# A hybrid decoder layer on one core: TensorE's auxiliary work put in program order and placed by counted turns

## The chip, the cores and the metric

The kernel runs on one core of one Trainium2 chip. The metric is the device time of one execution in microseconds (us); lower is better. In the profile PE is TensorE's matmul, PEld its weight load, DVE is VectorE, ACT is ScalarE, POOL is GpSimd and SP is SyncE, which here issues nearly all DMAs.

## The reference

One decoder layer on 256 tokens of width 2048, all float32. An RMSNorm and one wide input projection feed two mixers side by side: a Mamba-2 state space mixer (32 heads of 64, four groups with a state of 128, one chunk of 256 tokens) and a sparse attention (16 heads of 128, four key/value heads, compressed, selected and window branches). An output projection, a residual and a feed-forward block with a causal convolution follow. Inside the state space mixer xdt is x times dt, and cb holds the products of c and b.

```python
h = rms_norm(x, mix_norm_w[l])
proj = h @ w_in[l]
z, xbc, dt_raw, q, kc, vc, ksl, vsl, kwn, vwn, gl = jnp.split(proj, split_at, axis=-1)
xbc = jax.nn.silu(causal_depthwise_conv(xbc, ssm_conv_w[l], ssm_conv_b[l]))
xs, bm, cm = jnp.split(xbc, [D_SSM, D_SSM + SSM_GROUPS * SSM_STATE], axis=-1)
dt = jax.nn.softplus(dt_raw.astype(jnp.float32) + ssm_dt_bias[l].astype(jnp.float32))
y_ssm = ssd_chunked(xs.reshape(bsz, L, SSM_HEADS, SSM_HEAD_DIM), dt, ssm_a_log[l], ssm_d[l],
                    bm.reshape(bsz, L, SSM_GROUPS, SSM_STATE), cm.reshape(bsz, L, SSM_GROUPS, SSM_STATE))
y_ssm = rms_norm(y_ssm * jax.nn.silu(z), ssm_norm_w[l])
y_attn = nsa_attention(q.reshape(bsz, L, N_HEADS, HEAD_DIM), kv_shape(kc), kv_shape(vc),
                       kv_shape(ksl), kv_shape(vsl), kv_shape(kwn), kv_shape(vwn),
                       gl.reshape(bsz, L, 3, N_HEADS), cmp_pos_k[l], cmp_w1_k[l], cmp_w2_k[l],
                       cmp_pos_v[l], cmp_w1_v[l], cmp_w2_v[l])
y_attn = rms_norm(y_attn, attn_norm_w[l])
x = x + jnp.concatenate([y_attn, y_ssm], axis=-1) @ w_out[l]
h = rms_norm(x, ffn_norm_w[l])
u = causal_depthwise_conv(h @ w_up[l], ffn_conv_w[l], ffn_conv_b[l])
gate, val = jnp.split(u, 2, axis=-1)
x = x + (jax.nn.silu(gate) * val) @ w_down[l]
return rms_norm(x, final_norm_w)
```

## The kernel before

**The stream.** All large products are cut into steps. A step has one weight tile of 128x1024 floats: a DMA on SP's queue brings it (`raw`, four buffers), ScalarE rounds it to a high part (`whi`, line 338), VectorE takes the rest (`wlo`, line 344), and TensorE multiplies both parts. In the input projection a step is 24 matmuls of 256 columns, 16 with `whi` (line 368) and 8 with `wlo` (line 372); four steps make one pair of 128-channel outputs, which land in two of four `mm` banks of PSUM. In the output projection a step is 12 matmuls of 512 columns (lines 403 and 407). The plan of the input projection is b0 b1 c0 c1 x0 dt x1 ... x7, then the attention's keys and values, then q and z. The weights of a step are prepared three steps ahead (`AHEAD`), loads are issued seven ahead (`LOADS`).

**Evacuation.** When a pair is done its `post` runs. For b, c and x it is `conv_ssm` for each of the two channels: `u = mm * gate` (line 386, the root mean square of the input's tokens is in `gate`), one ScalarE multiply into `acc` (line 502), three VectorE multiply-adds (line 504), then a SiLU on ScalarE (line 531 for b and c, line 601 for x, where it writes `xs`). [...]

**Auxiliary work.** Between steps the loop calls `tick`, which advances the first of a queue of generators by so many yields: 2 for each step of b, c, dt and x, 1.45 for q and z, 1.5 for the state space mixer's later part (`R_SSM`, `RATE`). The generators hold the small products and transposes that run on TensorE between steps of the stream: `cb_group` (c.b for one group), `dt_softplus`, `make_xdt` (eight transposes of `xs` and a multiply by dt; the two token tiles t each with a bank of its own), `ssm_heads`, `attention(g)` (scores, softmax, transposes `trans` at line 835, products `pv` at lines 848 to 854, for t = 0 and 1), `split_attn` and `split_ssm`, and `x1_block`'s transposes after each quarter of the output projection (line 1024). A token's sum of squares is turned into a reciprocal root in `token_rsqrt` and `root_x`/`spread_root`.

**Order.** Instructions of each engine run in the order in which they stand in its queue. In the first six steps (while `pin` is set) that order is the program's. After it a list scheduler orders each engine's instructions; it hoists parts of an auxiliary burst into the matmul stream, and puts others back.

**The start.** Steps 0 to 2 are built with the transposes of x. `square_x(2)` stands behind step 3, `square_x(3)` and `root_x` behind step 4, `make_params` (six transposes of parameter rows, copied to `prm` and `dcol`) behind step 5, `spread_root` (the two products that fill `gate`) behind step 6, and there `pin` is cleared. The evacuation of b0 is put off from step 3 to step 6. `FILL` warm-up matmuls stand ahead of the first step.

Of the kernel before, what the change touches and what calls it, by code (L numbers as in the profile page):

```python
# [10 lines left out]
F32 = mybir.dt.float32  # L11
# [14 lines left out]
NHID = 256  # L26
NSH = 32
EPS = 1e-6
AHEAD, LOADS, WARM, FILL = 3, 7, 7, 4
RAWS, SPLITS, LATE = 4, 4, 4  # L30
R_SSM = 1.5
RATE = {"b": 2, "c": 2, "dt": 2, "x": 2, "ck": 1, "cv": 1, "q": 1.45, "z": 1.45}
PLAN = "b0 b1 c0 c1 x0 dt x1 x2 x3 x4 x5 x6 x7 kc0 kc1 vc0 vc1 ks0+ks1|ck vs kw0+kw1|cv vw " \
       "q0 q1 q2 q3 z0 z1 q4 q5 z2 z3 q6 q7 z4 z5 z6 z7"
NEG = -1e30
SCALE = 128 ** -0.5

# [5 lines left out]
def hymba_kernel(  # L43
# [6 lines left out]
    nc = tc.nc  # L50
# [12 lines left out]
    def big(slot, shape, dtype, name):  # L63
        return gp.tile(shape, dtype, tag=f"G{slot}", name=name)
# [13 lines left out]
    class Pinned:  # L78


        def __init__(self, eng):
            self.eng = eng

        def __getattr__(self, name):
            fn = getattr(self.eng, name)
            if not pin:
                return fn
            return lambda *a, **kw: tc.keep_in_program_order(fn(*a, **kw))  # L88

    pin = []  # L90
    V, A, T = Pinned(nc.vector), Pinned(nc.scalar), Pinned(nc.tensor)

    def split(hi, lo, src):
        A.activation(hi, src, AF.Copy)
# [330 lines left out]
    def dt_softplus(t80):  # L425
        dw = big(31, [NSH, 4, L], F32, "dtw")
        xb, m, z2, p_ = (dw[:, i] for i in range(4))
        ow = big(32, [NSH, 2, L], F32, "dtw2")
        e, ones_r = ow[:, 0], ow[:, 1]
        V.memset(ones_r, 1.0)  # L430
        A.activation(xb, t80[0:32], AF.Identity, bias=dtb)
        V.tensor_scalar(m, xb, 0.0, None, op0=ALU.max)
        A.activation(e, xb, AF.Abs)
        yield
        A.activation(e, e, AF.Exp, scale=-1.0)
        tc.keep_in_program_order(nc.scalar.activation(nA, nA, AF.Exp))
# [12 lines left out]
        yield  # L449
        V.scalar_tensor_tensor(p_, p_, 1.0, e, op0=ALU.add, op1=ALU.mult)  # L450
        V.scalar_tensor_tensor(m, p_, 2.0, m, op0=ALU.mult, op1=ALU.add)
        V.tensor_scalar(xb, m, nA, None, op0=ALU.mult)
        V.tensor_tensor_scan(e, ones_r, xb, 0.0, op0=ALU.mult, op1=ALU.add)
        A.dma_start(acum_d, e)
        yield
        ps = aux_bank()
        for t in range(NT):
            b = t * 144
            sl = slice(t * P, (t + 1) * P)
            T.transpose(ps[:, b:b + 32], m[:, sl], ident[0:32, 0:32])  # L460
            T.transpose(ps[:, b + 32:b + 64], e[:, sl], ident[0:32, 0:32])
            T.transpose(ps[:, b + 64:b + 144], t80[0:80, sl], ident[0:80, 0:80])
        pv = ps[:, 0:288].rearrange("p (t c) -> p t c", t=2)
        V.tensor_copy(tokp[:, :, 0:64], pv[:, :, 0:64])
        A.activation(gates, pv[:, :, 96:144], AF.Exp, scale=-1.0)
        V.tensor_scalar(gates, gates, 1.0, None, op0=ALU.add)
        V.reciprocal(gates, gates)
        V.tensor_scalar(gates[:, 0, 0:16], gates[:, 0, 0:16], t31, None, op0=ALU.mult)
        yield
# [41 lines left out]
    def cb_group(g):
        if g % 2 == 0:
            cbt.append(big(29 + g // 2, [P, 2, 384], F32, f"cbt{g // 2}"))
        for st in range(2):
            ps = aux_bank()
            b_ = bc[g][:, 0, :, st * P:(st + 1) * P]
            T.matmul(ps, b_[:, 0], bc[g][:, 1], start=True, stop=False)
            T.matmul(ps[:, 256:512], b_[:, 1], bc[g][:, 1, 0], start=False, stop=True)
            rt = t256("rt")
            cv = cbt[g // 2][:, g % 2]  # L520
            n = L - st * P
            A.activation(rt[:, :n], ps[:, 256 + st * P:512], AF.Copy)
            V.tensor_tensor(cv[:, 256 * st:256 * st + n], ps[:, st * P:256], rt[:, :n], op=ALU.add)
            V.tensor_tensor(cv[:, 256 * st:256 * st + P], cv[:, 256 * st:256 * st + P], tri, op=ALU.mult)
            yield

    def bc_evac(which, g0):
        def evac(c, ps):
            g = g0 + c
            acc = conv_ssm(ps, 16 + which * 4 + g)  # L530
            A.activation(acc, acc, AF.Silu)
            split(bc[g][:, which, 0], bc[g][:, which, 1], acc)
            if which == 1:
                aux.append(cb_group(g))
        return evac


# [3 lines left out]
    def make_xdt(i):  # L541
        xd = big(16 + i, [P, NT, 512], F32, f"xdt{i}")
        xdt.append(xd)
        for t in range(NT):
            ps = aux_bank()
            for j in range(4):
                T.transpose(ps[:, j * P:(j + 1) * P], xs[i][:, j, t * P:(t + 1) * P], ident)
            V.tensor_tensor(xd[:, t].rearrange("p (h e) -> p h e", e=64), ps.rearrange("p (h e) -> p h e", e=64),
                            dt_tok(t)[:, 8 * i:8 * i + 8].unsqueeze(2).to_broadcast([P, 8, 64]), op=ALU.mult)
            yield  # L550
# [207 lines left out]
    def attention(g):  # L758
# [126 lines left out]
        stats(1, p1[1], [2, 3])  # L885
        yield
        exps(1, 1)
        yield
        norm(1, p1[0], [0, 1])
        if g == 0:  # L890
            asq[0] = t256("asq", 1)
        yat[g] = big(12 + g, [P, 4, L], F32, f"yat{g}")
        a1 = trans(0, 1)
        exps(1, 2)
        yield
        a2 = trans(0, 2)
        exps(1, 3)
        yield
        po = aux_bank()
        a0 = trans(0, 0)  # L900
        norm(1, p1[1], [2, 3])
        pv(po, 0, 1, a1, True, False)
        yield
        pv(po, 0, 2, a2, False, False)
        prev = trans(1, 1)
        yield
        pv(po, 0, 0, a0, False, True)
        finish(po, 0)
        place_cmp(1)
        po = aux_bank()  # L910
        for b in (2, 3, 4, 0):
            nxt = trans(1, b)
            pv(po, 1, b - 1 if b else 4, prev, b == 2, False)
            prev = nxt
            yield
        pv(po, 1, 0, prev, False, True)
        finish(po, 1)
        yield

    def q_evac(pr):  # L920
        def evac(c, ps):
# [122 lines left out]
    def make_r2():  # L1044
        tot = const.tile([P, NT], F32, name="x1ss")
        V.tensor_reduce(tot, xsq, axis=AX.X, op=ALU.add)
        r2 = rsqrt_mean(tot, NT, "r2")
        yield
        ps = aux_bank()
        for t in range(NT):  # L1050
            T.matmul(ps[:, t * P:(t + 1) * P], r2[:, t:t + 1].to_broadcast([P, P]), ident, start=True, stop=True)
# [421 lines left out]
    for i in range(n):  # L1473
# [68 lines left out]
```

## Time and profile before

| | |
|---|---|
| time, 3 runs | median 1463.94 us (1463.76 to 1464.61) |
| the profiled execution | 1462.45 us, its span 1460.7 us |
| TensorE's mean granted clock | 0.998 |
| busy: PE, PEld, DVE, ACT | 1440.9, 1346.8, 1103.5, 844.2 us |
| instructions | 26504, of them 10512 matmuls on PE |

All times below are read in the profiled execution, from the start of its span. It took 1.75 us more than its span and 1.49 us less than the median. A row of the timeline gives the start of a group of like instructions, the time to the end of the last, engine, line, operation, output and inputs, shapes, count and, in brackets, the idle time ahead and who ended it. Ends of matmuls are modelled and overlap the next start, so that the pace of a stream is read from starts.

### The profile page before, as it was taken

The page shows a single profiled execution, that of the slowest core. Times are in us where ns is not written, and L with a number is a line of the kernel's source. Part 1 is how long each engine was busy: PE and PEld are TensorE (multiplying, and loading weights), DVE is VectorE, ACT ScalarE, POOL GpSimd, SP SyncE. Part 2 cuts the span into 40 slices and gives each one's busy share as a digit, 9 for nine tenths or more (in the row PEclk, how much of TensorE's full clock was granted, in tenths as well). Part 3 has the DMA queues.
Part 4 walks back from the last instruction along what each step waited for, and adds up shares of the span by engine and source line. Part 5 has one row for each costly group of instructions (what it writes and reads, how often), then busy time and mean ns, then how long its engine had stood idle before and what let it go on. Part 6 is the DMA issues. An engine that isn't in the chain of part 4 may idle for free.

```text
span 1460.7 us, 26504 instructions
## 1 busy us (share of the span) xinstructions
PE 1440.9 (99%) x10512; PEld 1346.8 (92%) x10512; DVE 1103.5 (76%) x1733; ACT 844.2 (58%) x1281; POOL 3.6 (0%) x19
## 2 busy tenths in 40 slices
PE   8999999999999999999999999999999999999997
PEld 8999999989999998888899999999999998788886
DVE  7899699756898898555476776776767778878777
ACT  6666456555676697444455555555555556555554
POOL 0000000000000000000000000000000000000000
PEclk9999999999999999999999999999999999999999
DMA  8667668775444446566556566666666565565664
GB/s 257 172 199 221 179 201 247 219 233 174 145 148 128 148 156 202 189 189 195 189 176 201 191 192 197 196 193 195 195 191 199 190 194 192 194 212 187 204 200 144
DMA packets 222701, 278.77 MB, mean 191 GB/s; under 512 B 13177, under 2 KB 186865, under 8 KB 222449
## 3 DMA queue, kind: packets, MB, share of 16 engines
q1 hardware_dynamic: 220800, 272.59, 59.6%
q10 hardware_dynamic: 1776, 4.50, 0.9%
q8 instruction: 82, 1.34, 0.4%
q14 instruction: 43, 0.34, 0.1%
HBM read 274.92 MB, written 2.13 MB: 190 GB/s over the span
## 4 chain that ended last, share of the span: by engine, by line
PE 90%; DVE 5%; ACT 3%; issue 1%; DMA 1%; DVEq 0%; ACTq 0%
PE mm L368 36%; PE mm L372 18%; PE mm L403 10%; PE mm L407 5%; PE aux L1142 4%; PE mm L1142 3%; PE aux L1145 2%; PE mm L1145 2%; PE mm L88 1%; DVE wlo L344 1%; DVE wlo L1174 1%; PE aux L1191 1%; PE aux L1190 1%; PE aux L585 1%; PE aux L1192 1%
## 5 line engine op out<-in xcount | busy, mean ns | idle before, releaser
L338 ACT ACTIVATE whi<-raw 128x1024 fp32r<-128x1024 f32 x408 | 431.4, 1058 | 428.3 <-PE mm L368 263.6
L344 DVE TENSOR_TENSOR wlo<-raw,whi 128x1024 fp32r<-128x1024 f32 x408 | 496.8, 1219 | 220.2 <-ACT whi L338 214.6
L368 PE MATMUL mm<-hcatf,whi 128*128 128x256 f32 x2816 | 348.6, 276 | 0.0
L368 PEld LDWEIGHTS mm<-hcatf,whi 128*128 128x128 f32 x2816 | 332.6, 188 | 0.1
L368 PE MATMUL mm<-hcat,whi 128*128 128x256 f32 x2192 | 279.2, 279 | 1.9 <-DVE u L386 1.9
L368 PEld LDWEIGHTS mm<-hcat,whi 128*128 128x128 f32 x2192 | 265.2, 188 | 4.5 <-issue 2.5
L372 PE MATMUL mm<-hcatf,wlo 128*128 128x256 f32 x1408 | 188.2, 276 | 0.0
L372 PEld LDWEIGHTS mm<-hcatf,wlo 128*128 128x128 f32 x1408 | 172.7, 188 | 0.0
L372 PE MATMUL mm<-hcat,wlo 128*128 128x256 f32 x1096 | 148.0, 277 | 0.0
L372 PEld LDWEIGHTS mm<-hcat,wlo 128*128 128x128 f32 x1096 | 135.6, 188 | 0.1
L1168 ACT ACTIVATE whi<-raw 128x1024 fp32r<-128x1024 f32 x88 | 91.6, 1056 | 67.8 <-DVE raw L1223 20.6
L1174 DVE TENSOR_TENSOR wlo<-raw,whi 128x1024 fp32r<-128x1024 f32 x88 | 105.7, 1219 | 13.0 <-ACT whi L1168 11.8
L403 PE MATMUL mm<-whi,ya 128*128 128x512 f32 x256 | 65.5, 394 | 0.0
L386 DVE TENSOR_TENSOR u<-mm,bc 128x256 f32<-128x256 f32 x88 | 37.2, 424 | 36.9 <-PE mm L372 35.7
L1142 PE MATMUL aux<-whi,act 128*128 128x512 f32 x256 | 63.4, 390 | 0.8 <-ACT whi L1168 0.8
L403 PE MATMUL mm<-whi,ys 128*128 128x512 f32 x256 | 63.2, 389 | 0.0
L1142 PE MATMUL mm<-whi,act 128*128 128x512 f32 x232 | 58.4, 389 | 0.0
L1142 PEld LDWEIGHTS aux<-whi,act 128*128 128x128 f32 x256 | 47.9, 188 | 11.2 <-ACT whi L1168 1.3
L403 PEld LDWEIGHTS mm<-whi,ys 128*128 128x128 f32 x256 | 48.1, 188 | 10.0
L403 PEld LDWEIGHTS mm<-whi,ya 128*128 128x128 f32 x256 | 47.3, 188 | 9.3
L1142 PEld LDWEIGHTS mm<-whi,act 128*128 128x128 f32 x232 | 43.6, 188 | 9.0
L799 ACT ACTIVATE p<-p,nm 128x256 f32<-128x256 f32 (+2 forms) x96 | 37.7, 394 | 3.0 <-DVE nm L783 1.4
(392 smaller groups left out, 1690.7 us busy)
## 6 DMA issues: line engine op xcount, KB each, us to landing
raw<-in_w_up_dram SPq DMA_DIRECT2D x176, 512.0 KB, 4.5
raw<-in_w_in_dram SPq DMA_DIRECT2D x160, 512.0 KB, 3.7
raw<-in_w_down_dram SPq DMA_DIRECT2D x88, 512.0 KB, 5.0
raw<-in_w_out_dram SPq DMA_DIRECT2D x64, 512.0 KB, 4.8
acq<-acum_d ACTq DMA_DIRECT2D x8, 512.0 KB, 4.7
raw<-in_cmp_w_k_dram SPq DMA_DIRECT2D x8, 512.0 KB, 4.4
raw<-in_cmp_w_v_dram SPq DMA_DIRECT2D x8, 512.0 KB, 4.4
x<-in_x_dram SPq DMA_DIRECT2D x4, 512.0 KB, 6.6
```

The costliest lines, as they stand in the source:

```text
L338: A.activation(hv, s.raw, AF.Copy)
L344: V.tensor_tensor(lv, s.raw, s.w[0].bitcast(F32), op=ALU.subtract)
L368: T.matmul(st["ps"][c], hv[:, kl, c * P:(c + 1) * P], k_of(k)[:, hl], start=(k == 0 and hl == 0), stop=False)
L372: T.matmul(st["ps"][c], lv[:, kl, c * P:(c + 1) * P], k_of(k)[:, 0], start=False, stop=(k == nk - 1))
L386: V.tensor_tensor(u, ps, root, op=ALU.mult)
L403: T.matmul(st["ps"][t], act(k)[:, hl, t * P:(t + 1) * P], hv[:, kl], start=(k == 0 and hl == 0), stop=False)
L407: T.matmul(st["ps"][t], act(k)[:, 0, t * P:(t + 1) * P], lv[:, kl], start=False, stop=(k == nk - 1))
L799: A.activation(v_, v_, AF.Exp, bias=nm[t][:, h, b:b + 1], accum_out=sm[t][:, h, b:b + 1])
L1142: T.matmul(x_[2 * t + n], act(k)[:, hl, t * P:(t + 1) * P], hv[:, n], start=(first and kl == 0 and hl == 0), stop=False)
L1145: T.matmul(x_[2 * t + n], act(k)[:, 0, t * P:(t + 1) * P], lv[:, n], start=False, stop=(last and kl == 1))
L1168: A.activation(hv[:, 0:n], src()[:, 0:n], AF.Copy)
L1174: V.tensor_tensor(lv[:, 0:n], src()[:, 0:n], s.w[0].bitcast(F32)[:, 0:n], op=ALU.subtract)
```

## The change

1. Every TensorE instruction keeps its program order for the whole kernel (`Pinned(..., True)`). ScalarE's and VectorE's order is still the scheduler's after the start.
2. Bursts that the scheduler used to move are placed by counted turns: `pause(n)` lets n yields pass first (`WAIT`). `cb_group` becomes `cb_pair` for two groups; `make_xdt` transposes both token tiles in one burst; the rates of q, z and the later state space part rise by 0.1.
3. In `attention`, `trans` results are held in a queue, and a product runs two turns behind its transposes.
4. The input's root: `square_x(2)`, `square_x(3)` and `root_x` stand behind step 3, `spread_root` behind step 5 and ahead of `make_params`; `pin` is cleared after step 6's evacuation, so that b0's evacuation is in program order on ScalarE and VectorE too. Two warm-up matmuls go. `split_attn`'s `token_rsqrt` moves behind `split_ssm`'s eighth piece.

```diff
-AHEAD, LOADS, WARM, FILL = 3, 7, 7, 4
+AHEAD, LOADS, WARM, FILL = 3, 7, 7, 2
-R_SSM = 1.5
-RATE = {"b": 2, "c": 2, "dt": 2, "x": 2, "ck": 1, "cv": 1, "q": 1.45, "z": 1.45}
+R_SSM = 1.6
+RATE = {"b": 2, "c": 2, "dt": 2, "x": 2, "ck": 1, "cv": 1, "q": 1.55, "z": 1.55}
+WAIT = {"bc": 7, "xdt": 2, "dt": 9, "r2": 9}
...
-    V, A, T = Pinned(nc.vector), Pinned(nc.scalar), Pinned(nc.tensor)
+    V, A, T = Pinned(nc.vector), Pinned(nc.scalar), Pinned(nc.tensor, True)
...
         A.dma_start(acum_d, e)
-        yield
+        yield from pause(WAIT["dt"])
         ps = aux_bank()
...
+    def cb_pair(g0):
+        yield from pause(WAIT["bc"])
+        cbt.append(big(29 + g0 // 2, [P, 2, 384], F32, f"cbt{g0 // 2}"))
+        todo = []
+        for g in (g0, g0 + 1):
+            for st in range(2):
+                ps = aux_bank()
...
-        for t in range(NT):
-            ps = aux_bank()
+        yield from pause(WAIT["xdt"] if i < 3 else 1)
+        banks = [aux_bank() for _ in range(NT)]
+        for t, ps in enumerate(banks):
             for j in range(4):
                 T.transpose(ps[:, j * P:(j + 1) * P], xs[i][:, j, t * P:(t + 1) * P], ident)
+        for t, ps in enumerate(banks):
...
+        for t, blk_ in ((0, 0), (1, 1), (1, 2), (1, 3), (1, 4), (1, 0)):
+            turn(t, blk_)
+            product()
...
     def split_attn():
-        rr["a"] = token_rsqrt(lambda t: asq[0][:, t * P:(t + 1) * P], "ra")
-        yield
...
             if k % 2 == 1:
+                yield
+            if k == 7:
+                rr["a"] = token_rsqrt(lambda t: asq[0][:, t * P:(t + 1) * P], "ra")
                 yield
...
         r2 = rsqrt_mean(tot, NT, "r2")
-        yield
+        yield from pause(WAIT["r2"])
...
         if i == 3:
-            square_x((2,))
-        elif i == 4:
-            square_x((3,))
+            square_x((2, 3))
             root_x()
         elif i == 5:
+            spread_root()
             make_params()
-        elif i == 6:
-            spread_root()
-            pin.clear()
         if s.post:
             s.post()
+        if i == 6:
+            pin.clear()
```

In the changed kernel every TensorE row has line 89, the helper that pins it, and other lines move by one to about eleven.

The first place is VectorE's queue around steps 6 to 8, where b0's evacuation stands; `u` frees a bank of the stream, and `bc_140` is the first group's b. Before, from the copy of `gate` on:

```order
L88 COPY gate<-aux 128x256
L344 TENSOR_TENSOR wlo<-raw,whi 128x1024
L386 TENSOR_TENSOR u<-mm,gate 128x256 x2
L344 TENSOR_TENSOR wlo<-raw,whi 128x1024
L504 SCALAR_TENSOR_TENSOR acc<-u,prm,acc 128x255 x2
L504 SCALAR_TENSOR_TENSOR acc<-u,prm,acc 128x254 x2
L504 SCALAR_TENSOR_TENSOR acc<-u,prm,acc 128x253 x2
L386 TENSOR_TENSOR u<-mm,gate 128x256 x2
```

The same place in the changed kernel, from the last `wlo` ahead of the first `u` on:

```order
L89 TENSOR_TENSOR wlo<-raw,whi 128x1024
L89 TENSOR_TENSOR u<-mm,gate 128x256
L345 TENSOR_TENSOR wlo<-raw,whi 128x1024
L89 SCALAR_TENSOR_TENSOR acc<-u,prm,acc 128x255
L89 SCALAR_TENSOR_TENSOR acc<-u,prm,acc 128x254
L345 TENSOR_TENSOR wlo<-raw,whi 128x1024
L89 SCALAR_TENSOR_TENSOR acc<-u,prm,acc 128x253
L89 TENSOR_TENSOR bc_140<-acc,bc_140 128x256
L89 TENSOR_TENSOR u<-mm,gate 128x256
```

Before, both `u` of b0 stood together ahead of the multiply-adds. Now the second `u` stands behind the whole evacuation of the first channel, its SiLU on ScalarE and its split into `bc_140`, and behind two `wlo`.

The second place is TensorE's queue at the end of x7, the last pair of x; `xs_1972` is the last block of four channels, and x6 and x7 wrote two of its channels each. Before:

```order
L368 MATMUL mm<-hcat_126,whi 128x256 x16
L372 MATMUL mm<-hcat_126,wlo 128x256 x8
L547 MATMUL aux<-ident,xs_1972 128x128 x4
L368 MATMUL mm<-hcat_123,whi 128x256 x16
L372 MATMUL mm<-hcat_123,wlo 128x256 x8
L368 MATMUL mm<-hcat_124,whi 128x256 x7
L547 MATMUL aux<-ident,xs_1972 128x128 x2
L368 MATMUL mm<-hcat_124,whi 128x256
L547 MATMUL aux<-ident,xs_1972 128x128 x2
L368 MATMUL mm<-hcat_124,whi 128x256 x8
```

The same place in the changed kernel, where the block is called `xs_1970`:

```order
L89 MATMUL mm<-hcat_126,whi 128x256 x16
L89 MATMUL mm<-hcat_126,wlo 128x256 x8
L89 MATMUL aux<-ident,xs_1970 128x128 x8
L89 MATMUL mm<-hcat_123,whi 128x256 x16
L89 MATMUL mm<-hcat_123,wlo 128x256 x8
```

Before, the two channels of x6 were transposed at once and those of x7 some 31 matmuls later, one at a time. Now all eight transposes stand right behind x7's last matmul. For the blocks of x3 and x5 the eight stand in one burst 24 matmuls, one step, behind the pair's last one.

The third place is TensorE's queue at the end of the output projection's first quarter, where `x_0` is the new residual and the transposes need it. The rows of before, then of the changed kernel:

```order
L407 MATMUL mm<-wlo,ys_6894 128x512 x4
L403 MATMUL mm<-whi,ya_6754 128x512 x3
L1024 MATMUL aux<-ident,x_0_6822 128x128 x2
L403 MATMUL mm<-whi,ya_6754 128x512 x2
L1024 MATMUL aux<-ident,x_0_6822 128x128 x2
L403 MATMUL mm<-whi,ya_6754 128x512 x3
```

```order
L89 MATMUL mm<-whi,ys_6908 128x512 x8
L89 MATMUL mm<-wlo,ys_6908 128x512 x4
L89 MATMUL aux<-ident,x_0_6807 128x128 x4
L89 MATMUL mm<-whi,ya_6739 128x512 x8
L89 MATMUL mm<-wlo,ya_6739 128x512 x4
```

Before, five matmuls of the next quarter stood between the last product of this one and its second pair of transposes. Now none do.

More of the change, by code (lines that the diff above doesn't have):

```diff
@@ L78, in hymba_kernel, with __init__ @@
     class Pinned:
-        def __init__(self, eng):
-            self.eng = eng
+        def __init__(self, eng, always=False):
+            self.eng, self.always = eng, always
         def __getattr__(self, name):
             fn = getattr(self.eng, name)
-            if not pin:
+            if not (pin or self.always):
                 return fn
@@ L509, in hymba_kernel, with pause @@
     cbt = []
[L511 to L514, printed above, removed]
-            ps = aux_bank()
-            b_ = bc[g][:, 0, :, st * P:(st + 1) * P]
-            T.matmul(ps, b_[:, 0], bc[g][:, 1], start=True, stop=False)
-            T.matmul(ps[:, 256:512], b_[:, 1], bc[g][:, 1, 0], start=False, stop=True)
+    def pause(n):
+        for _ in range(n):
+            yield
[6 more added lines that the diff above has]
+                ps = aux_bank()
+                b_ = bc[g][:, 0, :, st * P:(st + 1) * P]
+                T.matmul(ps, b_[:, 0], bc[g][:, 1], start=True, stop=False)
+                T.matmul(ps[:, 256:512], b_[:, 1], bc[g][:, 1, 0], start=False, stop=True)
+                todo.append((g, st, ps))
+        for g, st, ps in todo:
             rt = t256("rt")
@@ L532, in evac @@
             split(bc[g][:, which, 0], bc[g][:, which, 1], acc)
-            if which == 1:
-                aux.append(cb_group(g))
+            if which == 1 and c == 1:
+                aux.append(cb_pair(g0))
         return evac
@@ L543, in make_xdt @@
         xdt.append(xd)
-        for t in range(NT):
-            ps = aux_bank()
+        yield from pause(WAIT["xdt"] if i < 3 else 1)
+        banks = [aux_bank() for _ in range(NT)]
+        for t, ps in enumerate(banks):
             for j in range(4):
                 T.transpose(ps[:, j * P:(j + 1) * P], xs[i][:, j, t * P:(t + 1) * P], ident)
+        for t, ps in enumerate(banks):
             V.tensor_tensor(xd[:, t].rearrange("p (h e) -> p h e", e=64), ps.rearrange("p (h e) -> p h e", e=64),
@@ L887, in attention @@
         exps(1, 1)
+        exps(1, 2)
         yield
@@ L892, in attention, with turn, product @@
         yat[g] = big(12 + g, [P, 4, L], F32, f"yat{g}")
-        a1 = trans(0, 1)
-        exps(1, 2)
-        yield
-        a2 = trans(0, 2)
+        held = deque()
+        def turn(t, blk_):
+            held.append((t, blk_, trans(t, blk_)))
+        def product():
+            t, blk_, r = held.popleft()
+            first = blk_ == 1
+            if first:
+                pos[t] = aux_bank()
+            pv(pos[t], t, blk_, r, first, blk_ == 0)
+            if blk_ == 0:
+                finish(pos[t], t)
+        pos = [None, None]
+        turn(0, 1)
         exps(1, 3)
         yield
-        po = aux_bank()
-        a0 = trans(0, 0)
+        turn(0, 2)
         norm(1, p1[1], [2, 3])
-        pv(po, 0, 1, a1, True, False)
         yield
-        pv(po, 0, 2, a2, False, False)
-        prev = trans(1, 1)
-        yield
[L907 to L914, printed above, removed]
+        for t, blk_ in ((0, 0), (1, 1), (1, 2), (1, 3), (1, 4), (1, 0)):
+            turn(t, blk_)
+            product()
+            if (t, blk_) == (1, 2):
+                place_cmp(1)
             yield
-        pv(po, 1, 0, prev, False, True)
-        finish(po, 1)
-        yield
+        for _ in range(2):
+            product()
+            yield
     def q_evac(pr):
@@ L992, in split_attn @@
     def split_attn():
-        rr["a"] = token_rsqrt(lambda t: asq[0][:, t * P:(t + 1) * P], "ra")
-        yield
         for k in range(16):
@@ L1007, in split_ssm @@
             if k % 2 == 1:
+                yield
+            if k == 7:
+                rr["a"] = token_rsqrt(lambda t: asq[0][:, t * P:(t + 1) * P], "ra")
                 yield
@@ L1047, in make_r2 @@
         r2 = rsqrt_mean(tot, NT, "r2")
-        yield
+        yield from pause(WAIT["r2"])
         ps = aux_bank()
```

## The prediction

> **What bounds the kernel now.** I read the page first, then who waited for whom on TensorE, then the timeline at the places that the change touches. The page's busy line and the shares of the chain that ended last:
>
> ```profile
> PE 1440.9 (99%) x10512; PEld 1346.8 (92%) x10512; DVE 1103.5 (76%) x1733; ACT 844.2 (58%) x1281; POOL 3.6 (0%) x19
> PE 90%; DVE 5%; ACT 3%; issue 1%; DMA 1%; DVEq 0%; ACTq 0%
> L368 PE MATMUL mm<-hcatf,whi 128*128 128x256 f32 x2816 | 348.6, 276 | 0.0
> ```
>
> TensorE is the bound from end to end. So a TensorE queue that stands still costs its full time, and work elsewhere costs nothing unless TensorE comes to wait for it. The waits of TensorE, longest in total first (engine, line, whom it waited for: us, times, longest):
>
> ```profile
> PE mm L368 <- DVE u L386: 1.9, 1, 1.9
> PE aux L835 <- DVE p L813: 1.3, 2, 0.7
> PE aux L517 <- DVE bc L95: 1.1, 2, 0.8
> ...
> PE aux L460 <- DVE dtw L451: 0.7, 1, 0.7
> ...
> PE aux L1051 <- DVE r_r L167: 0.2, 1, 0.2
> ```
>
> The list has 14 rows, of which the first and the last are here; they sum to 10.1 us. That is the whole prize, and it is small. The unit of the stream is one step:
>
> ```profile
> 24.75 1.98 PE L88 MATMUL mm<-hcat,whi 128*128 128x256 f32 x16
> ...
> 26.57 1.07 PE L88 MATMUL mm<-hcat,wlo 128*128 128x256 f32 x8
> ...
> 27.47 0.67 PE L88 MATMUL aux<-ident,prow 120*128 120x120 f32 x6
> ```
>
> 24 matmuls from 24.75 to 27.47 are 2.72 us, 113 ns each from start to start, while the mean duration is 276 ns. So each time the stream is broken for an input that is late, up to 0.16 us of wait hide in the modelled end of the matmul before, and the list of waits reads low by about that much.
>
> **What the change removes.** (a) c.b: the two waits for `bc` (1.1 us) go, since `cb_pair` stands seven turns later, three or more steps behind its inputs; with two breaks of 0.16 that is 1.4. (b) dt: 0.7 us, and about five breaks between the transposes, 1.5. (c) `xdt`: before, the late transposes of x1, x3, x5 and x7 stood one or two at a time in the stream, about seven breaks, 1.1. (d) Attention. Busy time by stretches over the tails of the four groups (length, then PE, PEld, DVE, ACT, POOL busy, clock, DMA share, GB/s):
>
> ```profile
> 375.00:400.00 25.00, 24.78 (x193) 23.39 (x192) 19.15 (x32) 15.10 (x25) 0.00 (x0) 1.00 0.49 142
> 424.00:450.00 26.00, 25.93 (x204) 24.45 (x204) 19.89 (x34) 14.79 (x26) 0.00 (x0) 1.00 0.51 150
> 476.00:503.00 27.00, 26.32 (x208) 24.93 (x208) 23.20 (x40) 19.24 (x44) 0.00 (x0) 1.00 0.52 156
> 528.00:556.00 28.00, 26.51 (x207) 24.85 (x207) 26.94 (x53) 27.35 (x58) 0.00 (x0) 1.00 0.46 144
> ```
>
> PE stood idle 0.22 + 0.07 + 0.68 + 1.49 = 2.5 us, and some 13 breaks of 0.16 make it 4.5. A product two turns behind its transposes has a step or more for the copy, so I count it all. (e) The roots: the wait at line 1051 and its two breaks are 0.5, the first sum of squares of attention has two breaks, 0.3. Sum of the gains: 1.4 + 1.5 + 1.1 + 4.5 + 0.8 = 9.3 us. Ends: the waits alone, 1.1 + 0.7 + 2.5 + 0.2 = 4.5, and 12, should the breaks cost twice that.
>
> **What the change adds.** In program order TensorE can't slip the next matmuls under a late burst. Each burst of which the inputs come less than their latency behind the stream makes a wait that before was filled.
>
> *x.* What the pair x7 leaves, in the timeline of before:
>
> ```profile
> 161.15 0.88 DVE L386 TENSOR_TENSOR u<-mm,gate 128x256 f32<-128x256 f32 x2 [0.85 <-PE mm L372]
> 161.41 0.60 PE L547 MATMUL aux<-ident,xs 128*128 128x128 f32 x4
> ...
> 163.08 2.45 DVE L504 SCALAR_TENSOR_TENSOR acc<-u,prm,acc 128x255 f32<-128x255 f32 x6
> ...
> 165.23 0.81 ACT L601 ACTIVATE xs<-acc 128x256 f32<-128x256 f32 x2 [0.24 <-DVE acc L504]
> ```
>
> The stream reached its end at 161.41, and the second channel's SiLU ended at 165.23 + 0.81 = 166.04, 4.6 us later. Before, 31 matmuls of the next pair ran in that time. Now all eight transposes stand right behind x7, and four of them need the two late channels. Of the 4.6 us about 0.3 go under the transposes that can start: a loss of 4.3. For x5 the burst stands one step (2.72 us) behind the pair:
>
> ```profile
> 138.06 0.60 PE L547 MATMUL aux<-ident,xs 128*128 128x128 f32 x4
> ...
> 141.88 0.81 ACT L601 ACTIVATE xs<-acc 128x256 f32<-128x256 f32 x2 [0.24 <-DVE acc L504]
> ```
>
> 142.69 - 138.06 - 2.72 - 0.3 = 1.6. For x3 also one step, but there the state space part already uses ScalarE and VectorE, and a table load stands ahead of the SiLU:
>
> ```profile
> 115.28 0.60 PE L547 MATMUL aux<-ident,xs 128*128 128x128 f32 x4
> ...
> 120.05 1.28 ACT L601 ACT_TABLE_LOAD   x1 [0.22 <-DVE acc L504]
> ...
> 121.34 0.73 ACT L601 ACTIVATE xs<-acc 128x256 f32<-128x256 f32 x2
> ```
>
> 122.07 - 115.28 - 2.72 - 0.3 = 3.8; in the changed order the exponentials (`em`) still stand among these instructions, so I keep it. Together 9.7 us; from 1.6 + 1.6 + 4.3 = 7.5 (no `em` in the way) to 10.6 (nothing under the transposes).
>
> *The start.* Rows of before:
>
> ```profile
> 24.93 1.06 ACT L88 ACTIVATE whi<-raw 128x1024 fp32r<-128x1024 f32 x1 [3.92 <-DMA raw<-in_w_in_dram]
> ...
> 26.03 1.23 DVE L88 TENSOR_TENSOR wlo<-raw,whi 128x1024 fp32r<-128x1024 f32 x1 [2.91 <-ACT whi L88]
> ...
> 27.17 0.68 DVE L88 SCALAR_TENSOR_TENSOR xsqv<-x 128x512 f32<-128x512 f32 x1
> ...
> 29.71 0.16 DVE L88 TENSOR_REDUCE xss<-xpart 128x2 f32<-128x8 f32 x1
> ...
> 31.34 0.68 PE L88 MATMUL aux<-ident,r_r 128*128 128x128 f32 x4 [0.34 <-DVE r_r L88]
> ...
> 32.33 0.82 DVE L88 COPY prm<-aux 128x320 f32<-128x320 f32 x2
> 33.07 0.34 DVE L88 COPY dcol<-drow 64x16 f32<-64x16 f32 x2
> ...
> 36.61 2.09 PE L368 MATMUL mm<-hcat,whi 128*128 128x256 f32 x16 [1.85 <-DVE u L386]
> ...
> 41.27 0.42 ACT L531 ACTIVATE acc<-acc 128x256 f32<-128x256 f32 x1
> ```
>
> Both squares now follow the `wlo` of 26.03, at 27.17 and about 27.86, so that the sum comes near 28.65 instead of 29.71, and the root's product near 31.34 - 1.06 = 30.28. TensorE is there at 27.47 and waits 2.8 us. Two warm-up matmuls fewer bring nothing here: the chain hangs on the weights that land at 24.9. With root and parameter transposes behind it the stream goes on near 31.2, step 6 ends near 33.9 and step 7 near 36.6. On VectorE stand from 30.2 two `wlo` (starts 1.14 apart), gate (0.4), the parameter copies (1.1) and a `wlo`: the first `u` starts near 35.15. Another `wlo` (1.15) and two multiply-adds (0.4 each) reach 37.45. Then comes the `wlo` for a later step, which waits for step 7's last matmul and for ScalarE's `whi`, done near 37.2; it ends at 38.65, the third multiply-add at 39.05, the table load (1.28, as ahead of `xs`) later, SiLU and copy at 41.1, the split at 41.55 and the second `u` at 41.95. The third matmul of step 8 writes the bank that this `u` frees, and starts near 42.0 instead of 36.61: 5.4 us lost. Ends: 2 us (if the `wlo` in between are early and the first channel is not in the way) and 7.
>
> *The output projection.*
>
> ```profile
> 602.79 1.41 DVE L1031 SCALAR_TENSOR_TENSOR x<-mm,rs_r,x 128x512 f32<-128x512 f32 x2 [0.86 <-PE mm L407]
> ...
> 603.04 0.84 PE L403 MATMUL mm<-whi,ya 128*128 128x512 f32 x3
> ...
> 604.42 0.38 PE L1024 MATMUL aux<-ident,x 128*128 128x128 f32 x2
> ```
>
> The residual of the second token tile is ready at 602.79 + 1.41 = 604.20. Four transposes now stand at 603.04 and end near 604.5, a gap of 1.5 us for four transposes that cost about 0.5 when they were spread. So 1.0 more, in each of three quarters, and about 0.7 in the last: 3.7. Ends 2 and 5.
>
> *Attention in order.* The transposes of t = 1 stand 96 matmuls behind the last scores in groups 1 and 3 (120 before). Group 3 waited 0.7 for them at line 835; one step fewer, made up in part by products that now stand ahead: 1.5, from 0 to 4.
>
> *Free.* The new rates move bursts within the stream, where nothing waits for them; the loads of SP move two places ahead of the parameters', and step 6's weights land as before.
>
> *Sum.* 9.7 + 5.4 + 3.7 + 1.5 = 20.3 lost, 9.3 won: 11.0 us slower.
>
> **The clock.** Two of the new waits are longer than any in the stream so far. This trace has one idle time of that length, behind the last matmul (the last start is 1451.6):
>
> ```profile
> 1452.00:1455.60 3.60, 0.00 (x0) 0.00 (x0) 2.71 (x11) 2.60 (x8) 0.00 (x0) 1.00 0.46 151
> 1455.80:1460.70 4.90, 0.00 (x0) 0.00 (x0) 0.10 (x1) 0.00 (x0) 0.00 (x0) 0.50 0.61 209
> 1.11 3.36 PE L88 MATMUL aux<-warm_t 128*128 128x128 f32 x14 [1.11 <-DVE sqrt_set L118]
> ```
>
> The clock held for 3.6 us and was at a half from 3.9 on. At the start 14 warm-up matmuls took 3.36 us, 0.24 each, twice what instructions of the same shape take later (transposes of `xs`, four in 0.60 at 161.41 against two of `x` in 0.38 at 604.42: 0.11 for one more). If a clock lost in a wait comes back after as long a busy time, some 3.9 us of work run at half pace: 2 us each. The waits of 5.1 (start), 4.3 (x7) and 3.8 (x3) are near that limit; I take one loss, 2 us, from 0 to 6. [...]
>
> **The sum.** 11.0 + 2.0 = 13.0. The profiled execution took 1462.45 us, its span of 1460.7 and 1.75 around it, so the changed one would take 1475.4; the median of the runs is 1.5 above the profiled one, so I forecast 1476.9 us.
>
> **Rivals.**
> 1. *Faster.* The waits in order are short, because the scheduler gives ScalarE and VectorE another order where they are not pinned and the evacuation is quicker than in the old trace, and the start's second `u` does not hold the bank. For it: ScalarE is 58% and VectorE 76% busy. Against: the chain behind a pair (two `u`, two ScalarE multiplies, six multiply-adds of 0.4, two SiLUs) is serial. With the x waits at 3, the start at 0, the residual's at 2 and the rest gone it is 5 lost against 9.3 to 12 won: 1457 to 1460. It decides once the evacuation behind x7 takes under 2 us. Chance 0.13.
> 2. *No change within 0.2%* (about what a measurement of this kernel can tell): the lower ends of the losses (7.5 + 2 + 2 + 0) just over the gains: 1466. Chance 0.10.
> 3. *The clock falls at all three waits*, as said: 11.0 + 6 over the median, 1481. Chance 0.20.
> 4. *No fall at all*: 1475. It is in my own case's range. My case, with none or one or two falls, has 0.57.
>
> **How the numbers follow.** The likeliest case gives 1477. The range takes in the no change case below and three falls above, with 2 for the losses' upper ends: 1463 to 1484; left out are most of rival 1 and a little above. Faster by over 0.2%: rival 1, 0.13. Within 0.2% (1461.0 to 1466.9): 0.10. Slower: the rest, 0.77.
>
> **What would show it.** Right: on TensorE a wait near 4 us for `xs` right behind x7, ones near 4 and 1.6 in the steps behind x3 and x5, one near 5 us for `u` near 37 us, and about 1 us for the residual at three places; the waits for `bc`, `dtw` and `pt` gone; the third matmul of step 8 near 42.0. Wrong: if `xs` is ready before its burst, if TensorE's idle time in the start is no longer than before, or if the rows of granted clock show no fall (then 2 us are mine). A gain would have to show as PE idle time in the attention stretches falling by more than 4 us while the new waits stay under 5 in all.

## The result and the profile after

The changed kernel takes 1483.99 us (median of 4 runs, 1482.72 to 1484.83) against 1464.28 (4 runs, 1463.76 to 1465.06). The ratio is 1.0133, 95% interval 1.0116 to 1.0151: 19.7 us slower. In the batches of runs further down, single executions (one of the kernel before, two of changed ones) took 2081 to 3644 us and are left out of the medians here. The profiled execution took 1484.21 us, its span is 1482.5. The page's busy line and chain of the changed kernel:

```profile
PE 1447.6 (98%) x10508; PEld 1352.6 (91%) x10508; DVE 1105.0 (75%) x1733; ACT 844.6 (57%) x1281; POOL 3.6 (0%) x19
PE 88%; DVE 5%; DMA 3%; ACT 2%; issue 1%; SPq 0%; DVEq 0%; ACTq 0%
```

TensorE has the same matmuls but for two of the warm-up (two instructions each) and is 6.7 us busier: the same work ran slower in places. The rest of the span's 21.8 us is idle time. Its waits, longest in total first:

```profile
PE aux L89 <- ACT xs L612: 9.7, 3, 4.6
PE mm L89 <- DVE u L89: 4.7, 1, 4.7
PE aux L89 <- DVE r_r L89: 3.7, 1, 3.7
PE aux L89 <- DVE x L1048: 2.9, 8, 0.4
...
PE aux L89 <- DVE pt L96: 1.0, 1, 1.0
```

The rows for `xs`, `r_r` and `x` are bursts that now stand ahead of their inputs; the row for `u` is the stream itself, at step 8, whose bank the late evacuation frees. The waits for `bc`, `dtw` and `p` of before are gone. One wait for `pt` is left, of 1.0 us, where the prediction had it gone. The end of x7 in the timeline:

```profile
175.78 0.84 PE L89 MATMUL mm<-hcat,wlo 128*128 128x256 f32 x6
176.46 0.38 PE L89 MATMUL aux<-ident,xs 128*128 128x128 f32 x2
180.75 1.72 PE L89 MATMUL aux<-ident,xs 128*128 128x128 f32 x6 [3.91 <-ACT xs L612]
182.12 3.76 PE L89 MATMUL mm<-hcat,whi 128*128 128x256 f32 x16
```

Two transposes run, then TensorE stands until the SiLU of the late channels. The last row shows something else: 16 matmuls take 3.76 us, where they took 2.13 at the same place before. The clock had fallen. Stretches around the four falls ahead of the last matmul (length, then PE, PEld, DVE, ACT and POOL busy, and behind them the granted clock):

```profile
32.50:35.80 3.30, 3.30 (x17) 3.30 (x17) 3.25 (x7) 0.48 (x2) 0.00 (x0) 0.50 0.69 179
35.90:42.60 6.70, 3.87 (x33) 3.66 (x32) 4.09 (x7) 3.51 (x4) 0.00 (x0) 1.00 0.80 235
42.70:49.40 6.70, 4.92 (x23) 4.92 (x24) 4.30 (x11) 4.35 (x10) 0.00 (x0) 0.50 0.20 66
...
128.10:134.80 6.70, 4.76 (x22) 4.63 (x23) 6.66 (x12) 4.13 (x5) 0.00 (x0) 0.50 0.68 228
...
179.30:186.00 6.70, 5.25 (x24) 5.04 (x25) 2.66 (x6) 0.89 (x3) 0.00 (x0) 0.50 0.28 78
```

At half clock TensorE was busy for 3.30 + 4.92 + 4.76 + 5.25 = 18.2 us, so about 9.1 us of it is loss. That is the profiled execution, with a mean granted clock of 0.990; the other three had 0.993, 0.990 and 0.992, so the falls are not the same in each. The start of the changed kernel:

```profile
25.75 1.06 ACT L89 ACTIVATE whi<-raw 128x1024 fp32r<-128x1024 f32 x1 [4.84 <-DMA raw<-in_w_in_dram]
...
31.14 0.68 PE L89 MATMUL aux<-ident,r_r 128*128 128x128 f32 x4 [3.71 <-DVE r_r L89]
...
41.48 1.28 ACT L89 ACT_TABLE_LOAD   x1 [1.73 <-DVE acc L89]
...
44.01 0.42 DVE L89 TENSOR_TENSOR u<-mm,gate 128x256 f32<-128x256 f32 x1
...
44.48 1.86 PE L89 MATMUL mm<-hcat,whi 128*128 128x256 f32 x7 [4.71 <-DVE u L89]
```

The root's product waits 3.71 us, and the third matmul of step 8 starts at 44.48 instead of 36.92 (36.61 is the step's first), behind the table load, the first channel's split and the second `u`. Attention is where time came back; the same four tails as in the prediction, in the changed kernel:

```profile
387.00:412.00 25.00, 25.00 (x205) 24.18 (x204) 22.72 (x39) 17.92 (x41) 0.00 (x0) 1.00 0.52 154
437.00:462.00 25.00, 25.00 (x208) 24.20 (x207) 23.62 (x42) 19.32 (x47) 0.00 (x0) 1.00 0.57 168
488.00:515.00 27.00, 26.97 (x216) 25.68 (x215) 24.39 (x44) 21.62 (x46) 0.00 (x0) 1.00 0.53 152
544.00:573.00 29.00, 28.01 (x226) 26.70 (x225) 28.81 (x56) 27.91 (x57) 0.00 (x0) 1.00 0.52 163
```

PE idles 0.03 + 0.99 us in them, where it idled 2.5; the 0.99 is the wait for `pt`. The balance can be drawn up from the two traces by the start of the same matmul of the stream. The changed kernel's is later by

| matmul of the stream | later by, us | what lies between |
|---|---|---|
| 288 (end of c0) | 9.98 | the start |
| 528 (end of dt) | 8.08 | c.b: 1.9 won |
| 816 (end of x3) | 6.75 | dt: 1.3 won |
| 1500 | 21.06 | the three blocks of x: 14.3 lost |
| 3830 | 17.75 | attention: 3.3 won |
| 4800 | 21.87 | the residual's transposes: 4.1 lost |
| 8500 | 21.87 | nothing |

### The profile page after: what moved, and what is told of

Read it like the earlier page. It is cut to its first block, busy times and chain, and to the rows that moved or that the text cites. A ratio compares the mean times of both kernels' runs of the same rounds, so it can differ in the third digit from the quotient of the medians.

```text
span 1482.5 us, 26506 instructions
## 1 busy us (share of the span) xinstructions
PE 1447.6 (98%) x10508; PEld 1352.6 (91%) x10508; DVE 1105.0 (75%) x1733; ACT 844.6 (57%) x1281; POOL 3.6 (0%) x19
## 3 DMA queue, kind: packets, MB, share of 16 engines
HBM read 274.92 MB, written 2.13 MB: 187 GB/s over the span
## 4 chain that ended last, share of the span: by engine, by line
PE 88%; DVE 5%; DMA 3%; ACT 2%; issue 1%; SPq 0%; DVEq 0%; ACTq 0%
PE mm L89 77%; PE aux L89 11%; DMA raw<-in_w_in_dram 1%; DMA raw<-in_w_down_dram 1%; DVE wlo L345 1%; DVE wlo L1191 1%; DMA fnw<-in_final_norm_w_dram 1%; DVE acc L505 0%; DVE x L1048 0%; ACT p L810 0%; ACT whi L339 0%; DVE u L387 0%; DVE x L1387 0%; DVE sums L96 0%; DVE p L824 0%
## 5 line engine op out<-in xcount | busy, mean ns | idle before, releaser
L89 PE MATMUL mm<-hcat,whi 128*128 128x256 f32 (+1 forms) x2336 | 301.4, 282 | 4.8 <-DVE u L89 4.7
L89 PEld LDWEIGHTS mm<-hcat,whi 128*128 128x128 f32 (+1 forms) x2336 | 286.9, 191 | 7.7 <-DVE u L89 4.9
L89 PE MATMUL mm<-hcat,wlo 128*128 128x256 f32 (+1 forms) x1168 | 160.9, 278 | 0.0
L89 PEld LDWEIGHTS mm<-hcat,wlo 128*128 128x128 f32 (+1 forms) x1168 | 145.8, 189 | 0.2 <-DVE wlo L89 0.2
L1191 DVE TENSOR_TENSOR wlo<-raw,whi 128x1024 fp32r<-128x1024 f32 x88 | 105.8, 1221 | 11.6 <-ACT whi L1185 10.5
L89 PE MATMUL aux<-whi,act 128*128 128x512 f32 (+1 forms) x306 | 77.9, 387 | 1.1 <-ACT whi L1185 1.1
L89 PE MATMUL mm<-whi,act 128*128 128x512 f32 (+1 forms) x286 | 74.1, 386 | 0.0
L89 PEld LDWEIGHTS aux<-whi,act 128*128 128x128 f32 x306 | 57.0, 188 | 13.2 <-ACT whi L1185 1.5
L89 PEld LDWEIGHTS mm<-whi,act 128*128 128x128 f32 x286 | 53.5, 188 | 11.1
L89 PE MATMUL aux<-wlo,act 128*128 128x512 f32 (+1 forms) x153 | 43.6, 387 | 0.0
```

The costliest lines, as they stand in the source:

```text
L1191: V.tensor_tensor(lv[:, 0:n], src()[:, 0:n], s.w[0].bitcast(F32)[:, 0:n], op=ALU.subtract)
```

## The experiments

Theory A is the prediction's: TensorE in order waits for each burst by as much as its inputs' latency exceeds the distance at which the burst stands, and waits of that length make the clock fall. Rival B: keeping TensorE's order costs by itself, wherever the bursts stand. Rival C: the falls of the clock are not caused by these waits, or cost next to nothing.

**Later bursts for x.**

```diff
-        yield from pause(WAIT["xdt"] if i < 3 else 1)
+        yield from pause((2, 6, 4, 4)[i])
```

> The changed kernel with the bursts for the blocks of x3, x5 and x7 placed three, two and two steps behind their pairs instead of one, one and none. Theory A (waits in order for late inputs, and clock falls that these waits set off): the three waits for xs, 9.7 us in the changed kernel's trace, go, and with them the half-clock stretches that start at 128.0 and 179.2, which cost about half of 4.8 and of 5.3 us; so 1484.0 - 9.7 - 5.0 = 1469.3 us. Rival B (keeping TensorE's order costs by itself, wherever the bursts stand): 1482 or more. Rival C (the clock falls come by themselves and not from these waits): 1474, with half-clock stretches still near 128 and 179.

Measured: 1468.1 us (5 runs), ratio to before 1.0034 (1.0020 to 1.0047). The wait for `xs` is no longer in the list, and the clock falls only in the start (mean granted clock 0.995 in the profiled execution, 0.990 in the changed kernel's). The end of the step behind which the last burst now stands:

```profile
170.29 1.07 PE L89 MATMUL mm<-hcat,wlo 128*128 128x256 f32 x8
171.20 1.04 PE L89 MATMUL aux<-ident,xs 128*128 128x128 f32 x8
171.99 2.07 PE L89 MATMUL mm<-hcat,whi 128*128 128x256 f32 x16
```

Eight transposes in 0.79 us with no gap. A holds: 15.9 us were in three numbers of turns. B and C fall for this place.

**The start of before.**

```diff
-AHEAD, LOADS, WARM, FILL = 3, 7, 7, 2
+AHEAD, LOADS, WARM, FILL = 3, 7, 7, 4
...
-            square_x((2, 3))
+            square_x((2,))
+        elif i == 4:
+            square_x((3,))
             root_x()
         elif i == 5:
-            spread_root()
             make_params()
+        elif i == 6:
+            spread_root()
+            pin.clear()
         if s.post:
             s.post()
-        if i == 6:
-            pin.clear()
```

> The changed kernel with the start of before: square_x(3) and root_x behind step 4, make_params behind step 5, spread_root and the end of the pinned stretch ahead of step 6's evacuation, four FILL matmuls. Theory A: the stream is no longer 10 us behind at its 288th matmul, and the half-clock stretches at 32.4 and 42.7 are gone; 1484.0 - 10 = 1474.0 us. Rival C: the waits alone come back, 5.8, and 1478. A rival that the earlier root is worth its move: 1484 or more.

Measured: 1475.23 us, ratio 1.0082 (1.0067 to 1.0098). The new start costs 8.8 us. In this trace the stream is level with before at matmul 288 (0.1 us early), and the clock does not fall in the start (mean granted clock 0.996).

**Only the end of the pinned stretch.**

```diff
-        if s.post:
-            s.post()
         if i == 6:
             pin.clear()
+        if s.post:
+            s.post()
```

> The changed kernel, only that the pinned stretch ends ahead of step 6's evacuation, as before; the root stays two steps sooner. Theory A: both u of b0 come together again, the wait for u of 4.7 us shrinks to about 2 and no longer makes the clock fall (2.5 us of loss): 1484.0 - 2.7 - 2.5 = 1478.8 us; the wait for the root and the fall at 32.4 stay. Rival: the wait comes from the root's chain alone and stays: 1484.

Measured: 1476.35 us, ratio 1.0091 (1.0074 to 1.0108). That is 2.4 less than A gave, and 1.1 above the run with the whole start of before. VectorE and TensorE in this run's timeline:

```profile
34.49 1.23 DVE L89 TENSOR_TENSOR wlo<-raw,whi 128x1024 fp32r<-128x1024 f32 x1
35.63 0.75 DVE L387 TENSOR_TENSOR u<-mm,gate 128x256 f32<-128x256 f32 x2
...
36.54 1.07 PE L89 MATMUL mm<-hcat,wlo 128*128 128x256 f32 x8
37.45 1.75 PE L89 MATMUL mm<-hcat,whi 128*128 128x256 f32 x14
```

Both `u` stand together and are done near 36.4, ahead of step 8 at 37.45, so the wait doesn't shrink to 2 us, it is gone. I had put the wait of before there; but with the root's wait ahead of it the stream comes later, and the copy of `gate` sooner. The order of one evacuation was most of the start's loss: 7.6 of the 8.8 us by the medians. This trace is 0.7 us late at matmul 288, not 10; but behind its root's wait, of 2.6 us, the clock did not fall (the 16 matmuls from 31.90 on took 2.08 us, in the changed kernel 3.51), so that the loss behind the root, some 1.7 us in the changed kernel's trace, is missing from it.

**Work in the waits.**

```diff
+        if i in (1, 3):
+            busy = aux_bank()
+            for _ in range(36 if i == 1 else 30):
+                T.matmul(busy[:, 0:P], ident, ident, start=True, stop=True)
         banks = [aux_bank() for _ in range(NT)]
```

> The changed kernel with 36 idle matmuls of the identity (128 columns, 0.11 us each) put into the wait ahead of the burst for x3's block and 30 ahead of x7's: 3.9 and 3.3 us of work inside waits of 4.6 and 3.9, so that the stream is not later, but TensorE is not idle. Theory A: the waits' ends stay where they are, the clock does not fall at 128 and 179, and 2.4 + 2.6 us come back: 1479.0 us. Rival C, or the fall costs little: 1484.

Measured: 1484.83 us, ratio 1.0145 (1.0130 to 1.0161), no gain. The clock did not fall near 128 or 179: the 16 matmuls behind the two bursts took 2.14 and 2.13 us, in the changed kernel 3.71 and 3.76. But the filling was too long:

```profile
124.88 8.20 PE L89 MATMUL aux<-ident 128*128 128x128 f32 x72
132.92 1.04 PE L89 MATMUL aux<-ident,xs 128*128 128x128 f32 x8
```

Each of these matmuls is two instructions, so 36 of them took 8.0 us where 4.6 were free. That ate what the clock gave back, and the run tells nothing on the price of a fall. The same with half as many:

> The run with the idle matmuls again, with half as many: in float32 each of them ran as two instructions of 0.11 us, so that 36 and 30 took 8.0 and 6.7 us, longer than the waits that they were to fill. With 18 and 15 they take 4.0 and 3.4 us inside waits of 4.6 and 3.9. Theory A: the clock does not fall near 128 and 179 and 5.0 us come back against the changed kernel: 1479 us. Rival C (a fall costs next to nothing): 1484.

Measured: 1477.16, 1477.44 and 1480.82 us, ratio 1.0109 (1.0093 to 1.0125), 3.2 to 6.8 less than the changed kernel. The stretches of the two waits and behind them:

```profile
122.00:130.00 8.00, 7.66 (x66) 7.25 (x66) 8.00 (x18) 6.66 (x9) 0.00 (x0) 1.00 0.56 173
130.00:134.00 4.00, 4.00 (x38) 4.00 (x37) 3.46 (x5) 2.65 (x3) 0.00 (x0) 1.00 1.02 342
...
180.00:186.00 6.00, 6.00 (x55) 6.00 (x55) 2.81 (x3) 2.29 (x3) 0.00 (x0) 1.00 0.43 104
```

In this run's trace the three blocks of x lose 9.7 us from matmul 816 to 1500, where the changed kernel loses 14.3: the same stops, with 4.6 us of clock less. C falls: with TensorE busy for 7.66 of the 8 us around the first wait the granted clock was 1.00 there, as at the second, where the changed kernel had 0.50 behind both; a fall cost about 2.3 us here.

**The residual one step later.**

```diff
     def transpose_x1(c):
+        yield from pause(2 if c < 3 else 0)
         for kk in range(4):
```

> The changed kernel with the residual's transposes of the first three quarters of the output projection placed one step (12 matmuls) later. Theory A: the six waits of 0.3 to 0.4 us for x at these three places go and with them about 1.1 us each: 1480.6 us. Rival B: 1484.

Measured: 1481.15 us, ratio 1.0130 (1.0113 to 1.0147), 2.8 less than the changed kernel, with runs from 1479.41 to 1484.53. The trace shows no loss at the three places any more (matmuls 3830 to 4580: 0.6 us, against 4.0). That agrees with A. The times alone would not show a gain: the interval of this ratio and that of the changed kernel (1.0116 to 1.0151) lie on each other.

**No turns ahead of c.b.**

```diff
-WAIT = {"bc": 7, "xdt": 2, "dt": 9, "r2": 9}
+WAIT = {"bc": 0, "xdt": 2, "dt": 9, "r2": 9}
```

> The changed kernel with no counted turns ahead of the c.b bursts (7 before): they stand right behind the pairs c0 and c1. Theory A: a wait of what the evacuation takes in the changed kernel's trace, 57.6 to 63.5 and 69.9 to 75.6, so 5.9 and 5.7 us, each long enough for the clock to fall (2.5 each): 1484.0 + 11.6 + 5 = 1500 us (1495 to 1503). Rival (the wait is filled, since ScalarE and VectorE catch up at other places): 1488 or less.

Measured: 1498.26 us, ratio 1.0242 (1.0228 to 1.0257). The list of TensorE's waits and the first of the two stops:

```profile
PE aux L89 <- DVE bc L96: 10.7, 2, 5.4
```

```profile
56.90:62.20 5.30, 0.21 (x2) 0.01 (x1) 4.42 (x10) 2.80 (x7) 0.00 (x0) 1.00 0.68 198
62.30:65.50 3.20, 3.02 (x10) 2.66 (x11) 1.82 (x7) 1.12 (x4) 0.00 (x0) 0.50 0.00 0
65.70:72.00 6.30, 6.30 (x58) 6.30 (x57) 2.72 (x5) 2.13 (x2) 0.00 (x0) 1.00 0.18 30
```

Latency less distance gave 11.6 for the waits, measured 10.7, with the clock at 0.50 for 3.2 us behind the first. The rule gives a price at a place where it hadn't been fitted.

**Attention's tail of before.** The queue of products is taken out and the code of before put in its place, TensorE still in order.

```diff
-        for t, blk_ in ((0, 0), (1, 1), (1, 2), (1, 3), (1, 4), (1, 0)):
-            turn(t, blk_)
-            product()
...
+        for b in (2, 3, 4, 0):
+            nxt = trans(1, b)
+            pv(po, 1, b - 1 if b else 4, prev, b == 2, False)
+            prev = nxt
```

> The changed kernel with attention's tail of before (a product one turn behind its transposes, the last ones in the same turn), TensorE still in program order. Theory A: the queue of two turns is what wins the 3.8 us that the trace shows between matmuls 2450 and 3830, and program order makes the old tail's waits longer: 1488 us or more. Rival (the win comes from whole bursts, not from the distance): 1484.

Measured: 1493.59 us, ratio 1.0208 (1.0193 to 1.0223), 9.6 more than the changed kernel.

```profile
PE aux L89 <- DVE pt L96: 5.1, 7, 1.2
...
PE aux L89 <- ACT pt L95: 1.6, 1, 1.6
```

The old tail in order waits at eight places for the copies of its own transposes. Between matmuls 2450 and 3830 this trace loses 6.2 us on before, where the changed kernel wins 3.9. So program order needs the distance of two turns.

**TensorE's order free.**

```diff
-    V, A, T = Pinned(nc.vector), Pinned(nc.scalar), Pinned(nc.tensor, True)
+    V, A, T = Pinned(nc.vector), Pinned(nc.scalar), Pinned(nc.tensor)
```

> The changed kernel with TensorE's order given back to the scheduler behind the start; all counted turns, the product queue and the new start stay. Theory A: the scheduler puts the late transposes into the stream again, so the waits for xs (9.7, with 5.0 of clock) and most of those for x (3.5) go, about 2 us of broken stream come back: near 1468 us, with the start's loss of 10 still there. Rival (bursts placed by counts wait whoever orders the queue): 1482.

Measured: 1461.08 us (10 runs), ratio to before 0.9987 (0.9978 to 0.9997); 7 less than I expected, and 22.9 below the changed kernel: with the turns as they stand, program order alone costs more than the whole change. The scheduler fills most of the waits for `xs` and those for the residual, as A says, and it also fills most of the start:

```profile
PE aux L89 <- DVE r_r L89: 3.5, 1, 3.5
...
PE aux L557 <- ACT xs L612: 1.2, 1, 1.2
```

Its trace is 3.8 us late at matmul 288, not 10, with a root's wait of 3.5 us and one fall (mean granted clock 0.996), and no long wait for `u`. Attention keeps its win, 4.1 us between matmuls 2450 and 3830 (3.9 in the changed kernel), with the order pinned or free. The raised rates are in both, and no run takes them back, so the queue's share of that is not shown by itself. The ten executions also bear on C: the two with a granted clock of 0.999 took 1459.4 and 1459.5 us, those with 0.995 and 0.996 took 1462.2 and 1464.0.

**All three places mended.** The later bursts for x, the residual one step later and the start of before, TensorE in order:

> The changed kernel with the later bursts for x3, x5 and x7, the residual's transposes one step later and the start of before, all three together; pinned TensorE, the counted turns and the product queue stay. Theory A: 14.7 + 3.4 + 10 us less than the changed kernel: 1455.9 us, so 8 below the kernel before, which is what the change removes. Rival B: 1464 or more.

Measured: 1457.84 us (5 runs), ratio 0.9963 (0.9950 to 0.9976), 1.9 more than A gave and clear of B's 1464. The clock does not fall ahead of the last matmul (mean granted clock 0.998, as before), and the longest wait is

```profile
PE mm L89 <- DVE u L387: 1.6, 1, 1.6
```

With the early end of the pinned stretch in place of the whole start of before:

> The changed kernel with the later bursts for x3, x5 and x7 and the residual's transposes one step later, and with the pinned stretch ending ahead of step 6's evacuation while the root stays two steps sooner (in place of the whole start of before). Theory A: the start then costs 0.7 us against the kernel before, as in the run with the early end alone, so about the same as with the old start: 1457.8 us (1456 to 1459), and the earlier root is worth nothing either way. Rival: the earlier root's own wait of about 3 us still makes the clock fall: 1460 or more.

Measured: 1457.33 us (5 runs), ratio 0.9966 (0.9953 to 0.9979), the same. In its trace the root's wait of 2.3 us was followed by half clock for 3.4 us, so both statements of that expectation are half right: the time holds, the fall is there.

**The same, with TensorE's order free.**

> The kernel with later bursts, later residual transposes and the start of before, and with TensorE's order given back to the scheduler: whether program order by itself wins anything once the turns are right. Theory A: what program order wins is the broken stream, some 2 us, so 1460 us against 1457.8. Rival B (order costs by itself): 1456 or less. Rival D (all of the gain is order): 1463.

Measured: 1454.43 us (5 runs), ratio 0.9945 (0.9931 to 0.9959). Here A is wrong: I expected program order to win 2 us. The median is 3.4 below the pinned one, and its five executions (1454.0 to 1455.3) all lie below the five pinned ones (1456.6 to 1459.5). So B holds in this small measure: order costs some 3 us even with the turns right. One part is in the pinned traces: the eight transposes behind the last quarter of the output projection still wait there (0.7 us for the residual). Where the rest lies is open: there is no trace of this run to read it from. This is the fastest version, 8.6 us below the kernel before.

## Why the prediction was right, and where its sizes were off

*Direction and mechanism.* Right. The time is at the very top of the range (1484.0 against 1463 to 1484), and that it is still inside is luck: 13.0 us slower was the forecast, 19.7 were measured.

*x.* 9.7 us of waits predicted, 9.7 measured, but the equal sum is luck in part. For x3, x5 and x7 the prediction had 3.8, 1.6 and 4.3; the waits are 4.55, 1.19 and 3.91:

```profile
130.04 1.63 PE L89 MATMUL aux<-ident,xs 128*128 128x128 f32 x6 [4.55 <-ACT xs L612]
...
156.40 1.16 PE L89 MATMUL aux<-ident,xs 128*128 128x128 f32 x6 [1.19 <-ACT xs L612]
...
180.28 0.81 ACT L612 ACTIVATE xs<-acc 128x256 f32<-128x256 f32 x2 [2.46 <-DVE acc L505]
```

Behind x7 TensorE goes on at 180.75, with the first late channel, while I had priced by the end of the second (181.09). Behind x3 VectorE does 1.8 us of `em` between `u` and the multiply-adds (124.37 to 126.15), where before a `wlo` of 1.1 stood; that is most of the 0.75 which x3 waits longer. The run with later bursts removes all three. Of the 1.1 us that whole bursts were to win for x, 0.4 shows: these waits and half of 4.76 + 5.25 at half clock make 14.7, and 14.3 were lost.

*The start.* 5.4 predicted (5.1 from the third matmul's own 36.92); of the 9.98 measured some 4.1 are half of the busy time at half clock (3.30 + 4.92), so 5.9 are waits. The mechanism was right: the root waits, then the second `u` stands behind the first channel. The root waited 3.7 us, not 2.8: the weights that the prediction had land as before landed 0.8 us later (`whi` starts at 25.75, not 24.93). The rule that a moved root wins nothing is confirmed by the run with the early end, which is 1.1 us slower than the one with the whole start of before.

*The residual.* 3.7 predicted, 4.1 in the trace for all four quarters and the root behind them.

*Attention.* 4.5 won and 0.3 for the sums of squares, less 1.5 lost, 3.3 in all; 3.3 measured. Again the parts differ: no wait for `p` is left, so the 1.5 were not paid, and of the 2.5 us of idle time 1.0 stayed.

*c.b and dt.* 1.4 and 1.5 predicted, 1.9 and 1.3 measured.

*The clock* is the step that was mis-sized. I took one fall at 2.0 us; there were four, and half of 18.2 us is 9.1. Between the two profiled executions the span grew by 21.8 us, 8.8 more than the forecast 13.0, and 7.1 of the 8.8 are the clock; the other terms came to 12.7 instead of 11.0. Two things were wrong in it. I took the idle time at the end of the trace, 3.6 us without a fall, as the limit, so that the root's wait did not count; and I set 6 us as the upper end, 3.1 too low. The falls of the changed kernel start at 32.4, 42.7, 128.0 and 179.2 in the trace's clock records; the first lasts 3.4 us, the others 6.8. The first starts 1.3 us behind the root's wait of 3.71 us, the others within the waits of 4.71, 4.55 and 3.91. And 2.3 us of waiting were followed by half clock in one run, where 3.1 us in another were not. So the idle time at the end of one trace could not give a limit. All three long waits of the prediction lost the clock, and the root's as well.

*The rivals.* A quicker evacuation (1457 to 1460) did not come: SiLU ended 4.6 us behind x7 as before. Rival 3, a fall at each long wait, is what happened in the profiled execution, with the root's as a fourth and at a higher price than its 1481.

## What to carry to other kernels

When a queue is put in program order, the price of each burst can be read from the old trace: the latency from the last producer to the burst's last input, less the distance at which the burst will stand. Place by latency, not evenly: one or two steps more at three places were worth 16 us here. A long stop of TensorE should be priced with its clock as well: here half clock came with four stops of 3.7 to 4.7 us, and behind one of 2.3 us. Independent work placed in two of them, no longer than the stop, kept the granted clock at 1.00.

## What the runs showed of the hardware

The length of a wait did not tell by itself whether the clock fell. In the run with the early end and later bursts, this stretch was followed by half clock though TensorE was busy for 1.08 of its 3.4 us:

```profile
27.70:31.10 3.40, 1.08 (x10) 0.92 (x10) 2.93 (x13) 1.86 (x5) 0.00 (x0) 1.00 0.95 302
31.20:34.50 3.30, 3.30 (x18) 3.30 (x18) 3.29 (x7) 1.52 (x2) 0.00 (x0) 0.50 0.40 101
```

The wait in it was 2.3 us. In the run with the residual one step later the same wait was longer, 3.1 us, and the clock stayed at 1.00; TensorE was busy for 1.78 and 1.91 us of the two stretches across which it lies:

```profile
26.30:29.70 3.40, 1.78 (x16) 1.58 (x14) 2.67 (x6) 1.90 (x5) 0.00 (x0) 1.00 1.01 310
29.70:33.10 3.40, 1.91 (x18) 1.94 (x19) 3.07 (x9) 3.14 (x4) 0.00 (x0) 1.00 0.42 140
```

The kernel before kept its clock behind its longest wait, of 1.85 us, and the run with the early end alone behind the root's of 2.6 us. In the changed kernel four waits of 3.71, 4.71, 4.55 and 3.91 us came with half clock, and the one of 1.19 us did not. What decides between a wait of 2.3 us that lost the clock and one of 3.1 us that kept it, the runs do not show.
